# A recurrence in 32-frame chunks: values transposed for four chunks at a time, and operand copies placed behind the exponentials

## The chip, the core and the metric

The kernel runs on one core of a Trainium2 chip. The metric is the device time of one execution in microseconds; the time before is the median of three runs. A core has five engines that run side by side, each through a queue of its own in order: TensorE (PE in the profile, its weight loads PEld), VectorE (DVE), ScalarE (ACT), GpSimd (POOL) and SyncE (SP), which here only issues DMAs. Tiles lie in SBUF (128 partitions) or, where matmuls write, in the eight banks of PSUM.

## The reference, cut to what matters

One encoder block of width 1024 over 512 frames, all float32. Between two feed-forward halves stand two mixers; the change lies where both are computed side by side.

```python
def rwkv7_recurrence(r, w, k, v, a, b):
    # per head (8 heads of 64): S_t = S_{t-1} diag(w_t) + (S_{t-1} a_t) b_t^T + v_t k_t^T;  y_t = S_t r_t
    def step(state, inp):
        r_t, w_t, k_t, v_t, a_t, b_t = inp
        sa = jnp.einsum('bhvk,bhk->bhv', state, a_t)
        state = (state * w_t[:, :, None, :]
                 + sa[..., :, None] * b_t[:, :, None, :]
                 + v_t[..., :, None] * k_t[:, :, None, :])
        return state, jnp.einsum('bhvk,bhk->bhv', state, r_t)
    ...

def forgetting_attention(q, k, v, log_f):
    cum = jnp.cumsum(log_f, axis=-1)
    ...
    s = jnp.einsum('bhqd,bhkd->bhqk', q_i, k) * scale + c_i[..., :, None] - cum[..., None, :]
    pr = jax.nn.softmax(jnp.where(mask, s, -jnp.inf), axis=-1)
    return jnp.einsum('bhqk,bhkd->bhqd', pr.astype(v.dtype), v)

def reference(x, ...):
    x = x + 0.5 * swiglu(rms_norm(x, ffn1_norm), ...)
    p = rms_norm(x, mix_norm) @ w_in
    y_a = rwkv7_mixer(token_shift(p[..., :SHIFT_COLS]), ...) @ rwkv_proj
    y_b = fox_mixer(p[..., SHIFT_COLS:SHIFT_COLS + FOX_COLS], ...) @ fox_proj
    x = x + (gate_a * y_a + gate_b * y_b) @ w_out
    x = x + 0.5 * swiglu(rms_norm(x, ffn2_norm), ...)
    return rms_norm(x, final_norm)
```

## The kernel before

Activations lie with features on partitions and the 512 frames along the free dimension. Weights come in pieces from HBM (`raw`); each is split into a rounded half `whi` (a cast on ScalarE, line 133) and a remainder `wlo` (a subtraction on VectorE, line 134), and a wide product is three matmuls of 128x512, line 142. The program runs the first feed-forward half, the input projection, the scan (534 to 690 us), the output projections and the second half.

**The scan** (lines 1457 to 1539) runs the recurrence in 16 chunks of 32 frames, c = 0 to 15. The state of each pair of heads and the data that it meets lie in four sets of operands: `Rs` (64 rows of state, 32 rows of the solved values and 32 rows of V, by head) and `Ds`, both slices of the `RD` tiles. Chunk c uses set c % 4. Within a chunk TensorE makes, in this order:

- `xps`, what the state gives for the chunk's frames (issued by `read` at the end of the chunk before, line 1435), copied to `Xs` by VectorE;
- a staging transpose for two later chunks: in even chunks `stage_v` turns V (`vp`, line 1236, four transposes, one for each pair of heads) and ScalarE copies it in four copies into two sets `Rs` (line 1240); in odd chunks `stage_b` does the same for `Ds` (`bp`, lines 1245 and 1249);
- some of the wide products that are left over from the projections (`pq`, `pgt`, line 142), which fill the time;
- `ups`, the product with the chunk's inverse triangular matrix (line 1475), which ScalarE copies to `R` in four copies (lines 1479, 1480);
- more wide products, and the logits `lp` of one unit of the attention (lines 1308 to 1310);
- `sps`, the new state (line 1502), which VectorE scales by the decay into the next set (line 1504), and `yps`, the outputs (line 1508), copied over V by ScalarE (line 1512).

The attention works on 12 units, three for each pair of heads, spread over 12 of the chunks. For a unit VectorE takes maxima (`mx`, line 1318) and ScalarE exponentials (`pts`, line 1319) in one chunk; in the next, the weights are transposed by TensorE (line 1333), copied to `tr` (line 1338) and multiplied by the values (line 1347). Before a pair's first unit its queries and keys are squared, summed over a head (`pq2`, line 1161), rooted (`qrn`, lines 1165 and 1166) and scaled (line 1170), and `operands` copies them into the matmuls' operands (`qa`, `qb` on ScalarE, lines 1271 and 1272; `kb`, `klc` on VectorE). These copies, and the splits and evacuations of the wide products, stand in a list `side`, which `flush` empties at the start of each chunk.

The inverse triangular matrices are made ahead of the scan: 31 steps on VectorE (`TT`, lines 1122 and 1124), a DMA from ScalarE's queue to DRAM (`Td`, line 1125), and four DMAs back into `Tall` in another layout (line 1131), two on ScalarE's queue and two on GpSimd's.

`xps`, `vp`, `bp`, `ups`, `sps`, `yps` and most `pq2` share a pool `pr` of three PSUM banks, so that a new tile waits for the readers of the tile that had its bank before. The order of each engine's queue is set by a list scheduler when the program is built; what is marked `keep` stays in the order of the code, and `tc.issue_after(x)` puts the instructions of a block behind instruction x where both are on the same engine.

Of the kernel before, what the change touches and what calls it, by code (L numbers as in the profile page):

```python
# [9 lines left out]
F32 = mybir.dt.float32  # L10
F32R = mybir.dt.float32r
BF16 = mybir.dt.bfloat16
AF = mybir.ActivationFunctionType
# [5 lines left out]
P = 128  # L19
# [6 lines left out]
NP = DA // P  # L26
C = 32
NC = T // C
NB = T // P
# [22 lines left out]
def kernel(  # L52
# [7 lines left out]
    dve, act, pool, pe = nc.vector, nc.scalar, nc.gpsimd, nc.tensor  # L60
# [6 lines left out]
    pr = ctx.enter_context(tc.tile_pool(name="pr", bufs=3, space=PSUM))  # L67
# [11 lines left out]
    ident = cp.tile([P, P], F32, name="ident")  # L79
# [183 lines left out]
    with tc.tile_pool(name="x0", bufs=1) as x0:  # L263
        keep = tc.keep_in_program_order
# [436 lines left out]
    keep = tc.keep_in_program_order  # L701
# [180 lines left out]
    with ExitStack() as mx:  # L882
        rp = mx.enter_context(tc.tile_pool(name="rp", bufs=1))
        sctx = ExitStack()
        sp = sctx.enter_context(tc.tile_pool(name="sp", bufs=1))
# [48 lines left out]
        def normed(ps, rows=P):  # L934
            u = tmp("u")
            dve.tensor_tensor(u[0:rows, :], ps[0:rows, :], mix.rstd[0:rows, :], op=ALU.mult)
            return u

        u = normed(psa, 72)
        shifted(la, u, 64, PAR_MUA)  # L940
        dve.tensor_scalar(fz[64:72, :], u[64:72, :], pc(PAR_F)[64:72, :], None, op0=ALU.add)
        u = normed(psg, 96)
# [34 lines left out]
        vs = [V4[:, p] for p in range(NP)]  # L977
# [141 lines left out]
        for t in range(C - 1):  # L1119
            n, m = t + 1, C - 1 - t  # L1120
# [7 lines left out]
        for i in range(2):  # L1128
            for q in range(2):
                o = i * 64 + q * C  # L1130
# [59 lines left out]
        for b in range(NB):  # L1190
            o = vts[b]
# [30 lines left out]
        Rs, Ds = [RD[i // 2][:, i % 2] for i in range(4)], [RD[2 + i // 2][:, i % 2] for i in range(4)]  # L1222
        for q in range(2):
            pool.memset(Rs[0][half(q), :, q, :], 0.0)
            for i in range(4):
                o = (1 - q) * 64
# [3 lines left out]

        keep = tc.keep_in_program_order

        def stage_v(c, keep=keep):
            vp = pr.tile([P, NP, 2, 64], F32, tag="b", name="vp")
            for p in range(NP):
                keep(pe.transpose(vp[0:64, p].rearrange("p a b -> p (a b)"), vs[p][:, c * C:(c + 2) * C], ident[:]))
            for j in range(2):
                for q in range(2):
                    o = 32 + (1 - q) * 64
                    act.copy(Rs[(c + j) % 4][o:o + 32, :, q, :], vp[j * C:(j + 1) * C, :, q, :])  # L1240

        def stage_b(c, keep=keep):
            bp = pr.tile([P, NP, 2, 64], F32, tag="b", name="bp")
# [13 lines left out]
        def flush(budget):  # L1257
            while side and budget > 0:
                cost, do = side.pop(0)
                do()  # L1260
                budget -= cost
# [30 lines left out]
        class Unit:  # L1292
# [19 lines left out]
            def weights(s):  # L1312
                for q in range(2):
                    pt, mx = pts[:, q], pairs[s.p][2][q]
                    for b in s.bl:
                        n, mb = (b + 1) * P, mx[:, b:b + 1]
                        l = s.lps[q][:, s.at[b]:s.at[b] + n]
                        dve.tensor_reduce(mb, l, axis=AX.X, op=ALU.max, negate=True)
                        act.activation(pt[:, s.at[b]:s.at[b] + n], l, AF.Exp, bias=mb, accum_out=mx[:, NB + b:NB + b + 1])

            def scaled(s):
                for q in range(2):
# [103 lines left out]
        for part in (stage_v, stage_b):  # L1426
            part(0, lambda i: i)
        some_of = [(2, 1, 3), (3, 3, 2)] + [(2, 1, 3), (3, 1, 2), (4, 2, 2), (2, 1, 3), (2, 1, 3), (2, 1, 3)] + [(4, 2, 2), (2, 1, 3), (2, 1, 3), (2, 1, 3), (4, 3, 3), (2, 1, 3), (2, 1, 3), (2, 1, 3)]

        def read(c):  # L1430
            R = Rs[c % 4]
            xps = pr.tile([P, 2, 64], F32, tag="b", name="xps")
            for p, q in heads():
                o = (p // 2) * 64 + q * C
                keep(pe.matmul(xps[o:o + C, p % 2, :], G[p][q][:, c, 0, :], R[:, p, q, :], start=True, stop=True,
                               tile_position=(0, o)))
            Xs = sp.tile([P, 2, 64], F32, tag="Xs", name="Xs", bufs=2)
            return Xs, dve.tensor_copy(Xs[:], xps[:])
# [12 lines left out]
        def unit(n):  # L1451
            return units[places.index(n)] if n in places else None

        parted.extend((0, n, part) for n, part in enumerate(first_parts))
        with tc.issue_after(ahead.ins):
            Xs, taken = read(0)
        for c in range(NC):
            R, Rn, Dt = Rs[c % 4], Rs[(c + 1) % 4], Ds[c % 4]
            cs = slice(c * C, (c + 1) * C)
            u, v = unit(c - 1), unit(c)  # L1460
            n = some_of[c]
            late_logits = v and c == 12
            if c + 2 < NC:
                (stage_b if c % 2 else stage_v)(c + 2 - c % 2)
            with tc.issue_after(taken.ins):
                flush(100 if c in (1, 12) else 5)
            some(n[0])
            if u:
# [49 lines left out]
            if c + 1 < NC:  # L1518
                Xs, taken = read(c + 1)
# [249 lines left out]
```

## Time and profile before

| | before |
|---|---|
| median of three runs | 1140.15 us (1140.03 to 1140.36) |
| the profiled execution | 1140.51 us, its span 1138.8 us |
| granted TensorE clock over the span | 0.999 |
| scan | 534 to 690 us |

In the profile's groups an instruction stands with its line, engine and operation, output<-inputs, and sizes. In a timeline the columns are the start in us, the duration in us, engine, line, operation, tiles, sizes, the count of instructions merged, and in brackets how long the engine had been idle and what ended that. TensorE shows a float32 matmul of the recurrence as two, so that `xps` stands with x16 for 8 matmuls. The PE entries' durations overlap: the difference of two starts is what a matmul costs. A windows row gives start and end, the length, then busy time (and instructions) of PE, PEld, DVE, ACT and POOL, the granted clock, the DMA engines' share and GB/s. A waits row gives the engine and line that waited, who was waited for, the total, how often, and the longest. DMAs in a queue stand under ACTq and POOL.

### The profile page before, as it was taken

What the parts mean: (1) busy time and instruction counts of PE and PEld (TensorE: products, weight loads), DVE (VectorE), ACT (ScalarE), POOL (GpSimd) and SP (SyncE); (2) the same over time, 40 slices, a digit from 0 to 9 for tenths busy, and PEclk for the clock granted to TensorE, in tenths of its full rate; (3) what the DMA queues carried; (4) which work ended last, traced back from release to release, by engine and by line L of the source; (5) the groups of instructions that cost most, each with busy time, mean ns of one, the idle gap of its engine ahead of it and who ended that gap; (6) DMA issues with size and microseconds to landing.
All of it is one profiled execution on the core that took longest, in us unless ns stands there. A gap on an engine that the chain in (4) does not pass through costs nothing.

```text
span 1138.8 us, 19344 instructions
## 1 busy us (share of the span) xinstructions
PE 1127.8 (99%) x7674; PEld 988.1 (87%) x7674; DVE 830.0 (73%) x1301; ACT 600.9 (53%) x1004; POOL 106.8 (9%) x174
## 2 busy tenths in 40 slices
PE   9999999999999999999999999999999999999997
PEld 7899999988887888888777777888999999988887
DVE  6889999953246888777766668879999999943233
ACT  6645665532226754355877757536555566532121
POOL 2000000010111111321000011132000000010000
PEclk9999999999999999999999999999999999999999
DMA  8433333353334333345113236544333333363321
GB/s 260 135 93 109 97 112 111 95 181 115 112 103 124 103 104 103 112 142 139 38 38 100 67 113 200 177 142 126 103 97 108 111 94 112 107 192 91 89 78 74
DMA packets 210729, 131.14 MB, mean 115 GB/s; under 512 B 10415, under 2 KB 200943, under 8 KB 210639
## 3 DMA queue, kind: packets, MB, share of 16 engines
q1 hardware_dynamic: 202078, 108.67, 32.8%
q0 software_dynamic: 6320, 20.45, 5.4%
q8 instruction: 60, 0.98, 0.4%
q10 hardware_dynamic: 2240, 0.79, 0.3%
q14 instruction: 31, 0.25, 0.1%
HBM read 115.02 MB, written 14.88 MB: 114 GB/s over the span
## 4 chain that ended last, share of the span: by engine, by line
PE 96%; DVE 2%; ACT 1%; issue 1%; DVEq 0%; ACTq 0%
PE pd L142 21%; PE za L142 19%; PE zc L142 14%; PE pgt L142 8%; PE pk L142 6%; PE pw L142 4%; PE ppj L1553 4%; PE pb L142 3%; PE pa L142 3%; PE pq L142 3%; PE pv L142 2%; PE pl L142 1%; PE f L309 1%; PE gp L1076 1%; PE lp L1333 1%; PE lp L1347 1%
## 5 line engine op out<-in xcount | busy, mean ns | idle before, releaser
L133 ACT CAST whi<-raw 128x1024 fp32r<-128x1024 f32 (+3 forms) x117 | 113.8, 974 | 238.4 <-PE pd L142 153.7
L134 DVE TENSOR_TENSOR wlo<-raw,whi 128x1024 fp32r<-128x1024 f32 (+3 forms) x117 | 131.9, 1128 | 120.6 <-ACT whi L133 120.3
L142 PE MATMUL pd<-hh,wlo 128*128 128x512 f32 (+1 forms) x332 | 126.5, 381 | 0.0
L142 PE MATMUL pd<-hh,whi 128*128 128x512 f32 (+1 forms) x332 | 126.1, 380 | 0.0
L142 PE MATMUL pd<-hl,whi 128*128 128x512 f32 (+1 forms) x332 | 126.0, 379 | 0.0
L142 PE MATMUL zc<-xh,whi 128*128 128x256 f32 x296 | 83.8, 283 | 0.0
L142 PE MATMUL zc<-xl,whi 128*128 128x256 f32 x296 | 83.8, 283 | 0.0
L142 PE MATMUL zc<-xh,wlo 128*128 128x256 f32 x296 | 83.8, 283 | 0.0
L142 PEld LDWEIGHTS pd<-hl,whi 128*128 128x128 f32 x332 | 62.4, 188 | 12.0
L142 PEld LDWEIGHTS pd<-hh,whi 128*128 128x128 f32 x332 | 62.4, 188 | 11.7
L142 PEld LDWEIGHTS pd<-hh,wlo 128*128 128x128 f32 x332 | 62.4, 188 | 11.6
L142 PEld LDWEIGHTS zc<-xh,whi 128*128 128x128 f32 x296 | 56.8, 192 | 0.0
L142 PEld LDWEIGHTS zc<-xl,whi 128*128 128x128 f32 x296 | 56.8, 192 | 0.0
L142 PEld LDWEIGHTS zc<-xh,wlo 128*128 128x128 f32 x296 | 56.8, 192 | 0.0
L504 ACT CAST wtwo<-wsum 128x1024 fp32r<-128x1024 f32 x37 | 38.8, 1050 | 32.8 <-PE za L142 32.8
L142 PE MATMUL pgt<-xh,whi 128*128 128x512 f32 x128 | 53.0, 414 | 0.0
L507 DVE TENSOR_TENSOR wlo<-raw,whi 128x1024 fp32r<-128x1024 f32 x41 | 50.0, 1219 | 2.7 <-ACT whi L504 2.7
L516 DVE TENSOR_TENSOR wsum<-wsum,raw 128x512 f32<-128x512 f32 x74 | 50.9, 688 | 1.2
L516 DVE TENSOR_TENSOR wsum<-raw 128x512 f32<-128x512 f32 x74 | 50.6, 684 | 0.0
L142 PE MATMUL pgt<-xh,wlo 128*128 128x512 f32 x128 | 50.2, 392 | 0.0
L142 PE MATMUL pgt<-xl,whi 128*128 128x512 f32 x128 | 50.0, 391 | 0.0
L732 POOL DMA_DIRECT2D xP<-xpark x16 | 8.7, 548 | 438.2 <-PE za L142 437.5
(519 smaller groups left out, 3334.0 us busy)
## 6 DMA issues: line engine op xcount, KB each, us to landing
raw<-in_ffn_w_dram SPq DMA_DIRECT2D x118, 512.0 KB
raw<-in_w_in_dram SPq DMA_DIRECT2D x40, 512.0 KB
raw<-in_ffn_w_dram SPq DMA_DIRECT2D x15, 384.0 KB
xP<-xpark POOLq DMA_DIRECT2D x16, 256.0 KB, 4.7
raw<-in_w_out_dram SPq DMA_DIRECT2D x8, 512.0 KB
gsave<-gs SPq DMA_DIRECT2D x9, 256.0 KB
xin<-in_x_dram SPq DMA_DIRECT2D x4, 512.0 KB
xpark<-xT POOLq DMA_DIRECT2D x8, 256.0 KB, 6.3
```

What stands on the lines that cost most here:

```text
L133: marks["wide"] = act.copy(hi[:], raw[:])
L134: marks["rest"] = (eng or dve).tensor_tensor(lo[:], raw[:], hi[:].bitcast(F32), op=ALU.subtract)
L142: mm = pe.matmul(ps, w, x_, start=first and n == 0, stop=last and n == 2, skip_group_check=chain)
L309: return keep(pe.matmul(first[w][:], wt, x_[:], start=k == 0 and n == 0, stop=k == KD - 1 and n == 2))
L504: keep(act.copy(dst, src))
L507: keep(dve.tensor_tensor(dst, src, f32(hi), op=ALU.subtract))
L516: keep(dve.tensor_tensor(to, a, b, op=ALU.add))
L732: nc.gpsimd.dma_start(xT[c][:], xpark[c])
L1076: gm = pe.matmul(gps[g][o, c], BK[s, cc], G[p][q][s, cc], start=True, stop=True)
L1333: keep(pe.transpose(s.lps[q][:, k * P:(k + 1) * P], pts[:, q, k * P:(k + 1) * P], ident[:]))
L1347: keep(pe.matmul(av[half(q), j * P:(j + 1) * P], vt[k][:, h * 64:(h + 1) * 64], s.trs[q][:, o:o + P], start=k == 0, stop=k == b))
L1553: keep(pe.matmul(ps[:], a[:, k, :], y[k][b], start=k == 0 and n == 0, stop=k == NP - 1 and n == 2))
```

## The change

`stage_v` with c a multiple of four transposes V for four chunks (128 columns, so that `vp` fills all 128 partitions), copies the first two chunks' rows into `Rs` as before, and copies the upper 64 partitions of `vp` to a new SBUF tile `vkept` on VectorE. With the other even c it makes no transpose: ScalarE copies from `vkept` instead of `vp`. The second edit keeps, for each unit, its last exponential in `s.exp`, and puts what `flush` issues on ScalarE at the start of a chunk behind the last exponential of the unit of the chunk before.

```diff
+        vkept = []
+
         def stage_v(c, keep=keep):
-            vp = pr.tile([P, NP, 2, 64], F32, tag="b", name="vp")
-            for p in range(NP):
-                keep(pe.transpose(vp[0:64, p].rearrange("p a b -> p (a b)"), vs[p][:, c * C:(c + 2) * C], ident[:]))
+            if c % 4 == 0:
+                vp = pr.tile([P, NP, 2, 64], F32, tag="b", name="vp")
+                for p in range(NP):
+                    keep(pe.transpose(vp[:, p].rearrange("p a b -> p (a b)"), vs[p][:, c * C:(c + 4) * C], ident[:]))
+                src = vp
+            else:
+                src = vkept.pop()
             for j in range(2):
+                i = (c + j) % 4
                 for q in range(2):
                     o = 32 + (1 - q) * 64
-                    act.copy(Rs[(c + j) % 4][o:o + 32, :, q, :], vp[j * C:(j + 1) * C, :, q, :])
+                    act.copy(Rs[i][o:o + 32, :, q, :], src[i * C:(i + 1) * C, :, q, :])
+            if c % 4 == 0:
+                kept = sp.tile([P, NP, 2, 64], F32, name="vkept", tag="vkept")
+                dve.tensor_copy(kept[64:128], vp[64:128])
+                vkept.append(kept)
...
-                        act.activation(pt[:, s.at[b]:s.at[b] + n], l, AF.Exp, bias=mb, accum_out=mx[:, NB + b:NB + b + 1])
+                        s.exp = act.activation(pt[:, s.at[b]:s.at[b] + n], l, AF.Exp, bias=mb, accum_out=mx[:, NB + b:NB + b + 1])
...
-            with tc.issue_after(taken.ins):
+            with tc.issue_after(taken.ins), tc.issue_after(u.exp.ins) if u else ExitStack():
                 flush(100 if c in (1, 12) else 5)
```

The lines of the kernel after are numbered up to 11 higher than those before. In what follows, a row has its line, its operation, output<-inputs with the buffer's number, and the size of what is written.

TensorE, start of chunk 4, before: the last of `xps`, the transposes of V for chunks 6 and 7, and the wide products of a projection of the queries and keys (`pq`).

```order
L1435 MATMUL xps<-RD_5172,G_3630 32x64
L1435 MATMUL xps<-RD_5172,G_3631 32x64
L1236 MATMUL vp<-ident,V_3792 64x128 x4
L142 MATMUL pq<-xh_3591,whi 128x512
L142 MATMUL pq<-xl_3592,whi 128x512
```

The same place in the kernel after:

```order
L1446 MATMUL xps<-RD_5172,G_3630 32x64
L1446 MATMUL xps<-RD_5172,G_3631 32x64
L142 MATMUL pq<-xh_3591,whi 128x512
L142 MATMUL pq<-xl_3592,whi 128x512
L142 MATMUL pq<-xh_3591,wlo 128x512
```

The transposes are gone, and with them a tile of the pool `pr`; so it is in chunks 0, 8 and 12. Otherwise the order on TensorE is the same.

ScalarE, chunks 7 and 8, before: from the copies of chunk 7's `ups` to the table load that the first gate needs. `whi` and the four copies to `qa` and `qb` come from `flush`, the two exponentials are those of chunk 7's unit.

```order
L133 CAST whi<-raw 128x1024
L1338 COPY tr<-lp 128x384 x2
...
L1480 COPY RD_5173<-ups 32x2x64
L1271 CAST qa_6192<-qk_5395 64x512
L1272 CAST qb_5195<-qk_5395 64x512
...
L1319 ACTIVATE pts,mx_5721<-lp,mx_5721 128x512
L1319 ACTIVATE pts,mx_5722<-lp,mx_5722 128x512
L1165 ACTIVATE qrn<-pq_6140,epsr 128x512
L1166 ACTIVATE qrn<-qrn 128x512
L1512 COPY V_3792<-yps 128x4x32
L1371 ACT_TABLE_LOAD
L1371 ACTIVATE gs<-gs 128x512
L1240 COPY RD_5173<-vp 32x4x64 x4
```

The same stretch after:

```order
L1349 COPY tr<-lp 128x384 x2
...
L1491 COPY RD_5173<-ups 32x2x64
L1330 ACTIVATE pts,mx_5720<-lp,mx_5720 128x512
L1330 ACTIVATE pts,mx_5721<-lp,mx_5721 128x512
L133 CAST whi<-raw 128x1024
L1282 CAST qa_6188<-qk_5392 64x512
L1283 CAST qb_5195<-qk_5392 64x512
...
L1165 ACTIVATE qrn<-pq_6136,epsr 128x512
L1247 COPY RD_5173<-vkept 32x4x64
L1523 COPY V_3792<-yps 128x4x32
L1247 COPY RD_5173<-vkept 32x4x64
L1166 ACTIVATE qrn<-qrn 128x512
L1382 ACT_TABLE_LOAD
```

The cast and the operand copies have moved behind the exponentials, and two of the four copies for chunks 10 and 11 stand ahead of the table load (the other two stand earlier, in chunk 7). Chunks 3 and 4 have changed in the same way; in chunk 2 a `whi` has moved from ahead of the `tr` copies to behind the exponentials of that chunk.

ScalarE, ahead of the scan, before: the inverse's way through DRAM (`Td`, `Tall`), among the squares of the first pair (`qsq`, `shi`) and splits and evacuations.

```order
L133 CAST whi<-raw 128x1024
L1146 COPY qk_5044<-pq 128x512
L1125 DMA Td<-TT 128x1024
L1155 ACTIVATE qsq<-qk_4978 128x512
L1155 ACTIVATE qsq<-qk_5011 128x512
L157 CAST shi<-qsq 128x512 x2
L1131 DMA Tall<-Td 32x32x32 x2
L133 CAST whi<-raw 128x1024
L1146 COPY qk_5077<-pq 128x512
```

After:

```order
L133 CAST whi<-raw 128x1024
L1146 COPY qk_5044<-pq 128x512
L1247 COPY RD_5173<-vkept 32x4x64 x4
L1125 DMA Td<-TT 128x1024
L1155 ACTIVATE qsq<-qk_4978 128x512
L1155 ACTIVATE qsq<-qk_5011 128x512
L157 CAST shi<-qsq 128x512 x2
L133 CAST whi<-raw 128x1024
L1146 COPY qk_5077<-pq 128x512
L1131 DMA Tall<-Td 32x32x32 x2
```

The four copies for chunks 2 and 3, which stood behind the first `xps` of the scan, now stand ahead of `Td`, and `Tall` stands behind a cast and a copy. On VectorE the last step of the inverse has moved behind a `wlo`, before:

```order
L1122 TENSOR_TENSOR prod<-TT,Ls 128x31
L1124 TENSOR_TENSOR TT<-TT,prod 128x31
L1153 TENSOR_TENSOR qk_4978<-qk_4978,rstd 128x512
L1153 TENSOR_TENSOR qk_5011<-qk_5011,rstd 128x512
L1206 SCALAR_TENSOR_TENSOR nf<-la,nf 8x512
L134 TENSOR_TENSOR wlo<-raw,whi 128x1024
```

and after:

```order
L1122 TENSOR_TENSOR prod<-TT,Ls 128x31
L134 TENSOR_TENSOR wlo<-raw,whi 128x1024
L1124 TENSOR_TENSOR TT<-TT,prod 128x31
L1153 TENSOR_TENSOR qk_4978<-qk_4978,rstd 128x512
L1153 TENSOR_TENSOR qk_5011<-qk_5011,rstd 128x512
L1206 SCALAR_TENSOR_TENSOR nf<-la,nf 8x512
```

That `wlo` waits for the `whi` of the first row of the ScalarE listing.

## The prediction

> **What bounds the kernel now.** I read the page's busy shares first, then the chain that ended last, then the busy time of each engine in the stage that the change touches, which is the scan (534 to 690 us), and last TensorE's own waits there.
>
> ```profile
> span 1138.8 us, 19344 instructions
> PE 1127.8 (99%) x7674; PEld 988.1 (87%) x7674; DVE 830.0 (73%) x1301; ACT 600.9 (53%) x1004; POOL 106.8 (9%) x174
> ...
> PE 96%; DVE 2%; ACT 1%; issue 1%; DVEq 0%; ACTq 0%
> ```
>
> ```profile
> 534.00:690.00 156.00, 153.78 (x1620) 120.89 (x1619) 105.87 (x233) 119.77 (x303) 11.93 (x21) 1.00 0.27 81
> ```
>
> ```profile
> PE xps L1435 <- DVE RD L1504: 1.0, 4, 0.5
> ```
>
> The reader is to see that TensorE (PE) is the bound: 99% of the span, 96% of the chain. The scan is the one stage with something to collect, and it is little: in its 156.00 us TensorE is busy 153.78, VectorE (DVE) 105.87, ScalarE (ACT) 119.77. So two things make the kernel shorter here: fewer TensorE instructions, and fewer of the waits in the missing 2.2 us. The largest group of these waits, 1.0 us in four, is `xps` waiting for the decayed state of the chunk before; the change touches nothing in that chain. ScalarE, at 77% of the stage, is the engine to watch when its queue is put in another order.
>
> **The change part by part.** *Four transpose groups go.* `stage_v` is called eight times; of its groups of four transposes, those of chunks 2, 6, 10 and 14 (issued in chunks 0, 4, 8 and 12) are gone.
>
> ```profile
> 534.01 0.44 PE L1435 MATMUL xps<-RD,G 128*32 128x64 f32 x16
> 534.38 0.62 PE L1236 MATMUL vp<-ident,V 128*64 128x128 f32 x4
> 534.77 0.48 PE L142 MATMUL pq<-xh,whi 128*128 128x512 f32 x1
> 535.08 0.39 PE L142 MATMUL pq<-xl,whi 128*128 128x512 f32 x1
> ```
>
> ```profile
> 669.73 0.44 PE L1435 MATMUL xps<-RD,G 128*32 128x64 f32 x16
> ...
> 670.44 0.40 PE L142 MATMUL pgt<-xl,whi 128*128 128x512 f32 x1
> ```
>
> From the start of `xps` to the second wide matmul behind it, chunk 0 takes 535.08 - 534.01 = 1.07 us with a `vp` group between, and chunk 14, which has none, 670.44 - 669.73 = 0.71. The difference of starts, 0.36 us, is what a group costs (its 0.62 us of busy time overlap its neighbours). Four of them: **-1.44 us**, all on the path, since TensorE has no slack to absorb them.
>
> *The four groups that stay become wider*, 128 columns of V as weights in place of 64. No `vp` row shows that shape, but `bp`, the other staging transpose, has it.
>
> ```profile
> 542.64 0.66 PE L1245 MATMUL bp<-ident,BK 128*128 128x128 f32 x4
> 543.06 0.48 PE L142 MATMUL pq<-xh,whi 128*128 128x512 f32 x1
> ```
>
> ```profile
> L1236 PEld LDWEIGHTS vp<-ident,V x32: 108/111/113, 489.2 to 648.8; 128*64 128x64 f32 x32
> ...
> L1240 ACT COPY RD<-vp x32: 360/363/365, 497.1 to 650.3; 32x256 f32<-32x256 f32 x32
> ```
>
> ```profile
> L1245 PEld LDWEIGHTS bp<-ident,BK x32: 138/141/143, 495.2 to 661.3; 128*128 128x128 f32 x32
> ```
>
> A `bp` group takes 543.06 - 542.64 = 0.42 us from its start to the next matmul's, a `vp` group 534.77 - 534.38 = 0.39. So 0.03 a group, four groups: **+0.12 us**. The weight load itself grows from 111 to 141 ns; if none of that were covered it would be 16 x 30 ns = 0.48, which is the upper bound, and zero the lower.
>
> The Trainium skill, page "TensorE: Matmul & The Clock Gate", section on LDWEIGHTS, has a load's time grow with its columns, P / 1.2 ns. By that 64 more columns are 53 ns, 0.85 us for 16 transposes, and the sum below would be -1.14 instead of -1.87. The trace does not agree: its two loads differ by 30 ns, and the groups by 0.03 us.
>
> *A wait in chunk 4 goes.* The `vp` group of chunk 4 takes its PSUM bank over from the head sum whose root is `qrn`, and `qrn` stands on ScalarE behind a weight cast, four operand copies and two exponentials.
>
> ```profile
> 572.22 0.45 PE L1435 MATMUL xps<-RD,G 128*32 128x64 f32 x16
> 573.17 0.63 PE L1236 MATMUL vp<-ident,V 128*64 128x128 f32 x4 [0.51 <-ACT qrn L1165]
> ```
>
> From `xps` to `vp` are 0.95 us here against 0.37 in chunk 0: 0.58 lost. The group is gone, and the bank's next user is the state product `sps` at the end of chunk 4. **-0.58 us.** What is late next there is `qrn` itself, since the cast and the copies now stand between the exponentials and it; nothing asks for the bank before that `sps`, so this is free. If something did, 0.58 would come back.
>
> *A wait in chunk 2 goes.* The second logits matmul needs the bank that `tr` empties, and a weight cast `whi` stood ahead of `tr`.
>
> ```profile
> 555.91 1.03 ACT L133 CAST whi<-raw 128x1024 fp32r<-128x1024 f32 x1
> 556.97 0.48 ACT L1338 COPY tr<-lp 128x384 f32<-128x384 f32 x1
> ```
>
> ```profile
> 557.29 0.23 PE L1310 MATMUL lp<-dmask,identb 128*128 128x128 bf16 x1
> 557.50 0.45 PE L1308 MATMUL lp<-kb,qa 128*128 128x384 f32 x1
> ...
> 557.96 0.23 PE L1310 MATMUL lp<-dmask,identb 128*128 128x128 bf16 x1
> 558.00 0.48 PE L142 MATMUL pq<-xh,whi 128*128 128x512 f32 x1
> ```
>
> `tr` ends at 557.45 and the matmul starts at 557.50, 0.21 after its forerunner, where the like step costs 0.04. In the new order the cast stands behind the exponentials of chunk 2 and `tr` comes a microsecond sooner: **-0.17 us**. The casts themselves are hidden: the order of their remainders `wlo` on VectorE hardly moves, and each new place of a `whi` is still ahead of it.
>
> *The inverse is read back later.* The scheduler also moves rows ahead of the scan. The last step of the triangular inverse now waits on VectorE behind a `wlo`, and on ScalarE the four kept copies go ahead of the write `Td`, and a cast and a copy ahead of half of its reading back `Tall`.
>
> ```profile
> 523.01 1.05 ACT L133 CAST whi<-raw 128x1024 fp32r<-128x1024 f32 x1 [3.91 <-PE pq L142]
> 523.42 0.35 ACTq L1125 DMA_DIRECT2D Td<-TT  x1
> 523.97 0.58 ACT L1146 COPY qk<-pq 128x512 f32<-128x512 f32 x1
> ...
> 526.41 1.03 ACTq L1131 DMA_DIRECT2D Tall<-Td  x2
> ...
> 529.41 0.57 ACT L1146 COPY qk<-pq 128x512 f32<-128x512 f32 x1
> ```
>
> ```profile
> 525.28 1.23 DVE L134 TENSOR_TENSOR wlo<-raw,whi 128x1024 fp32r<-128x1024 f32 x1
> ```
>
> ```profile
> 526.68 1.60 POOL L1131 DMA_DIRECT2D Tall<-Td  x2 [2.34 <-DMA Td<-TT]
> ```
>
> ```profile
> DMA to landing us min/median/max: 6.2/6.2/6.3
> ```
>
> ```profile
> 537.27 0.46 PE L1475 MATMUL ups<-Xs,Tall 64*64 64x64 f32 x8
> ```
>
> VectorE: cast done at 524.06, `wlo` 1.23, the last step about 0.2, so 525.5. ScalarE: copy done at 524.55, four kept copies at 0.363 (the `vp` copies' price), so `Td` goes out at 526.0 in place of 523.42, 2.6 later. GpSimd's (POOL's) two reads follow it by the same: 529.3 and 530.1, landing at 536.3. ScalarE's two go out behind the copy that ends at 529.98. The first user, `ups`, comes at 537.27 - 0.36 = 536.9. So **0**, with 0.6 us left of a margin that was 3.6 (the before's last read landed at about 533.7); upper bound, with reads half a microsecond to one slower, +0.6.
>
> *ScalarE's fullest stretch becomes longer.* In chunks 7 and 8 its queue runs without a gap into the state copies that `sps` needs.
>
> ```profile
> 606.40 1.29 DVE L1318 TENSOR_REDUCE mx<-lp 128x1 f32<-128x512 f32 x2 [1.12 <-PE lp L1310]
> ```
>
> ```profile
> 606.81 0.61 ACT L1271 CAST qa<-qk 64x512 fp32r<-64x512 f32 x1
> ...
> 609.13 0.69 ACT L1319 ACTIVATE pts<-lp,mx 128x512 f32<-128x512 f32 x1
> ...
> 609.81 0.68 ACT L1319 ACTIVATE pts<-lp,mx 128x512 f32<-128x512 f32 x1
> ...
> 610.48 0.68 ACT L1165 ACTIVATE qrn<-pq,epsr 128x512 f32<-128x512 f32 x1
> ...
> 618.47 0.26 ACT L1480 COPY RD<-ups 32x128 f32<-32x128 f32 x1
> ```
>
> ```profile
> 619.14 0.34 PE L1502 MATMUL sps<-RD,RD 128*64 128x64 f32 x4
> ```
>
> Before, the copies end at 618.73 and `sps` starts at 619.14: 0.4 us of slack. Now the exponentials stand first and cannot start before the maxima: the second maximum is there at 607.69, its exponential done at 608.4. Then the cast (about 1.0), the operand copies (609.13 - 606.81 = 2.32), and the rest of the queue (618.73 - 610.48 = 8.25) with two kept copies in place of four `vp` copies (-2 x 0.363): 619.2. `sps` would come at 619.14 - 0.36 = 618.8, and its second half, which needs the last copies, a quarter of a microsecond later. **+0.2 us**, between 0 and 0.6. A kept copy is priced like a `vp` copy although its source is SBUF; no row shows that one, and the smaller copy from PSUM (0.26) and the operand cast from SBUF with twice the elements (0.61) bound it.
>
> The Trainium skill, page "VectorE: DVE Perf Modes", section on SBUF-source ops, puts ScalarE's fixed cost 52 cycles of 1.2 GHz higher from SBUF than from PSUM; by that two kept copies are 0.09 us longer and the sum is -1.78. No row before shows such a copy.
>
> *The four new copies on VectorE* (64x512 from PSUM to `vkept`; no row shows one, and the 1.23 of a `wlo` of twice the elements is a safe upper bound) cost nothing: those in the scan stand ahead of a wait for logits like the 1.12 in the row above; the first lies inside the inverse, whose end is set by the cast of 523.01. Without that cover they would delay the maxima by half of 1.23 each.
>
> Sum: -1.44 + 0.12 - 0.58 - 0.17 + 0 + 0.2 = **-1.87 us**. The profiled execution took 1140.51 (span 1138.8 and 1.7 around it), so 1138.64; the median of the runs, 1140.15, is 0.36 under it, so **1138.3**. That is 0.16%, and about 0.2% (2.3 us) is what a measurement of this kernel can tell from no change.
>
> **The rivals.** *The decay waits shrink too*: if less work ahead on ScalarE and VectorE let the state come sooner, the 1.0 us of `xps` waits goes as well: -2.87, 1137.3. Against it: in chunks without value products nothing but `sps` and its decay stands between, and neither is changed. *Only the transposes count*: the two waits come back elsewhere, since the queue is as full as before, or the moved rows are not ahead of what waits: -1.44 + 0.12 + 0.2 = -1.12, 1139.0. For it: ScalarE's 77%. Against: the banks' next users are far off. *The wider weight load shows in full*: 0.48 in place of 0.12, 1138.7; the groups of `bp` speak against it, and it is the page's rule on LDWEIGHTS in this kernel's numbers. *The inverse comes late*, the one way to slower: every microsecond that `Tall` lands after 536.9 stops TensorE for one at the first `ups`. If the reads took 9.3 us in place of 6.2, they land at 539.4, a stall of 2.5, and the kernel takes 1140.8. It outweighs the gain from a landing at 538.8 on, and is slower by 0.2% from 541.1. The margin of 0.6 speaks for it; against it, the DMA share of 0.27 in the scan leaves the reads room.
>
> **How the numbers follow.** Forecast 0.54, the decay waits 0.14, only the transposes 0.18, the full weight load 0.05, the late inverse 0.09. The range takes in the first two rivals, the full load, the bounds of the last two terms and the late inverse up to about no change: 1137.0 to 1140.2. Faster by over 0.2% (under 1137.87) needs the second case or the forecast at its lower edge, with no stall in chunk 8 and no wider transposes: 0.28. Slower by over 0.2% needs the late inverse at its worst: 0.05. Within: 0.67.
>
> **What would show it.** The scan's TensorE rows: `xps` directly followed by wide matmuls in chunks 0, 4, 8 and 12; `vp` groups at 0.42 from start to start; no wait for `qrn` in chunk 4 and no 0.21 step in chunk 2; the exponentials of chunk 7 done near 608 (less what TensorE has gained); `sps` of chunk 8 waiting 0.2 us or so for the copies; `Td` out near 526.0, `Tall` landing by 536.3 and `ups` not waiting. The forecast is wrong if `ups` waits, if chunk 8 waits more than 0.6, or if the scan's end moves by less than 1 us or more than 2.5.

## The result, and the profile after

| | before | after |
|---|---|---|
| median of 20 runs each | 1140.55 us (1140.03 to 1141.82) | 1138.56 us (1138.05 to 1139.72) |
| ratio, with its 95% interval | | 0.9982 (0.9976 to 0.9988) |
| profiled execution, its span | 1140.51, 1138.8 | 1139.03, 1137.3 |
| the scan, first to last `xps` | 144.83 us | 142.78 us |

The kernel is 1.99 us shorter, 0.18%; the forecast was 1.87. (The forecast of the time, 1138.3, started from a median of three runs of before, which lies 0.40 under that of the 20.) The page of the changed kernel, its busy shares, and the windows row of its scan (columns as before; the row begins at the first `xps` and ends at 689.20, so its length is not to be compared with the 156.00 of before):

```profile
span 1137.3 us, 19322 instructions
PE 1126.4 (99%) x7658; PEld 986.7 (87%) x7658; DVE 834.0 (73%) x1305; ACT 602.3 (53%) x1004; POOL 106.9 (9%) x174
```

```profile
534.63:689.20 154.57, 152.87 (x1606) 120.08 (x1606) 108.23 (x237) 120.03 (x300) 11.97 (x22) 1.00 0.27 83
```

TensorE has 16 matmuls fewer (the four groups), VectorE four copies more, 2.8 us; the rest has hardly changed. The profiled execution shows only 1.5 us of the 2.0, because the one of after began later: its first `xps` stands at 534.63, before's at 534.01, and the whole of that was there already at the first wide product (23.01 against 22.36). So the two traces are compared within the scan. TensorE's instructions have the same order in both, the `vp` groups aside (and two `yps` of chunk 8, which start ahead of the last `sps`). For each I take its start after minus its start before; where this shift changes, time was won or lost. It goes from +0.62 at the first `xps` to -1.43 at the last.

| place | forecast | change of the shift |
|---|---|---|
| chunks 0, 4, 8, 12: a group gone | -0.36 each | -0.38 each |
| chunks 2, 6, 10: wider group | +0.03 each | +0.03 each |
| chunk 2, second logits matmul | -0.17 | -0.17, and -0.02 at the next |
| chunk 4, wait for `qrn` | -0.58 | -0.58 (-0.96 with the group) |
| chunk 8, ahead of the logits | 0 | -0.10 |
| chunk 8, `sps` | +0.2 | +0.21 |
| scan | -1.87 (with the group ahead of it) | -2.05 |

The -0.38 of a group are read at the first wide product behind it. The second product gives 0.02 to 0.03 back, so that by the forecast's own measure, from `xps` to the second product, a group was worth 0.35 to 0.36. In `sps` of chunk 8 the shift rises by up to 0.27, at a late `yps`, and 0.06 of that come back at the next product; so the lasting loss is 0.21, where the expectations of two runs below speak of 0.25.

The rows of after that answer to those shown of before, on TensorE in chunks 0, 2, 4 and 8:

```profile
534.63 0.44 PE L1446 MATMUL xps<-RD,G 128*32 128x64 f32 x16
535.00 0.50 PE L142 MATMUL pq<-xh,whi 128*128 128x512 f32 x1
...
537.55 0.46 PE L1486 MATMUL ups<-Xs,Tall 64*64 64x64 f32 x8
...
557.64 0.23 PE L1321 MATMUL lp<-dmask,identb 128*128 128x128 bf16 x1
557.68 0.42 PE L1319 MATMUL lp<-kb,qa 128*128 128x384 f32 x1
...
572.36 0.45 PE L1446 MATMUL xps<-RD,G 128*32 128x64 f32 x16
572.74 0.50 PE L142 MATMUL pq<-xh,whi 128*128 128x512 f32 x1
...
617.87 0.84 PE L1513 MATMUL sps<-RD,RD 128*64 128x64 f32 x15
618.49 0.25 PE L1519 MATMUL yps<-G,RD 128*64 128x32 f32 x2
618.54 0.22 PE L1513 MATMUL sps<-RD,RD 128*64 128x64 f32 x1
```

Behind `xps` stands a wide product at once in chunks 0 and 4, 0.37 and 0.38 later; the second logits matmul of chunk 2 follows its forerunner by 0.04; and in chunk 8 the 16 matmuls of `sps` are drawn out to 0.84 us (0.69 where nothing is waited for), since they start one after another as ScalarE's copies of `ups` come in. These are on ScalarE, with what stands ahead of them:

```profile
606.23 0.69 ACT L1330 ACTIVATE pts<-lp,mx 128x512 f32<-128x512 f32 x1 [0.17 <-DVE mx L1329]
...
611.54 0.40 ACT L1247 COPY RD<-vkept 32x256 f32<-32x256 f32 x1
611.95 0.27 ACT L1523 COPY V<-yps 128x128 f32<-128x128 f32 x1
612.23 0.40 ACT L1247 COPY RD<-vkept 32x256 f32<-32x256 f32 x1
...
618.01 0.26 ACT L1491 COPY RD<-ups 32x128 f32<-32x128 f32 x1
```

No other row of this stretch has an idle time: from the exponential at 606.23, which waited 0.17 us for its maximum, to the end of the last copy at 618.27 the queue is full. The kept copies' prices, which no row of before showed, from the tile's view:

```profile
L1247 ACT COPY RD<-vkept x16: 400/403/407, 525.2 to 647.9; 32x256 f32<-32x256 f32 x16
L1250 DVE COPY vkept<-vp x4: 694/694/695, 499.3 to 632.1; 64x512 f32<-64x512 f32 x4
```

The inverse, its last step on VectorE and its write `Td`, before:

```profile
523.12 0.22 DVE L1124 TENSOR_TENSOR TT<-TT,prod 128x31 f32<-128x31 f32 x1
```

and after:

```profile
525.86 0.21 DVE L1124 TENSOR_TENSOR TT<-TT,prod 128x31 f32<-128x31 f32 x1
```

```profile
526.16 0.36 ACTq L1125 DMA_DIRECT2D Td<-TT  x1
526.43 0.41 ACT L1247 COPY RD<-vkept 32x256 f32<-32x256 f32 x1
```

`Td` goes out at 526.16, which is 525.54 on before's scale (forecast 526.0). It follows the end of VectorE's last step by 0.09 us, as before by 0.08. The four kept copies, which stand ahead of it in ScalarE's queue, did not hold it: the fourth starts 0.27 us later than the write. GpSimd's second read goes out at 531.4 and lands 4.2 us later, at 535.6. `ups` comes at 537.55 and does not wait.

### The profile page after: what moved, and what is told of

The parts are those of the page before. It is cut to its first block, busy times and chain, and to the rows that moved or that the text cites. A ratio compares the mean times of both kernels' runs of the same rounds, so it can differ in the third digit from the quotient of the medians.

```text
span 1137.3 us, 19322 instructions
## 1 busy us (share of the span) xinstructions
PE 1126.4 (99%) x7658; PEld 986.7 (87%) x7658; DVE 834.0 (73%) x1305; ACT 602.3 (53%) x1004; POOL 106.9 (9%) x174
## 4 chain that ended last, share of the span: by engine, by line
PE 97%; DVE 2%; DMA 1%; ACT 0%; issue 0%; SPq 0%; DVEq 0%
PE pd L142 21%; PE za L142 19%; PE zc L142 14%; PE pgt L142 8%; PE pk L142 6%; PE pw L142 4%; PE ppj L1564 4%; PE pq L142 3%; PE pb L142 3%; PE pa L142 3%; PE pv L142 2%; PE pl L142 1%; PE gp L1076 1%; PE sps L1513 1%; PE lp L1344 1%; PE f L309 1%
```

## The experiments

All are compared by the scan, first to last `xps`, each read from one profiled execution. How much the scan of one kernel differs from execution to execution was not tried; where an edit touches nothing, the shift between two of these traces stays the same within some 0.05 us over whole chunks. The times, whose ratios are to the kernel before, hardly tell effects under a microsecond apart.

**The transposes alone.** The second edit is undone.

```diff
-            with tc.issue_after(taken.ins), tc.issue_after(u.exp.ins) if u else ExitStack():
+            with tc.issue_after(taken.ins):
```

> The transposes of four chunks and the kept buffer alone; the operand copies stay ahead of the exponentials as in the kernel before. The measure is the scan from the first to the last xps matmul: 144.82 us before, 142.78 with both edits. Theory (each term belongs to the edit that the prediction gave it to): the four groups go, 0.38 each, the stall of 0.58 in chunk 4 goes with its group, the wider groups cost 0.03 each, and the 0.17 in chunk 2 and the 0.10 ahead of the logits in chunk 8 stay: -2.0, less what the state product of chunk 8 waits. If the full ScalarE queue makes that wait, it is 0.2 here too and the scan takes 143.0; if the new order makes it, it is 0 and the scan takes 142.8. Rival (the stall in chunk 4 left because of the order): it stays, and the scan takes 143.4 to 143.6. Time 1138.7 +- 0.3 by the theory, 1139.3 by the rival.

The scan took 143.85 us, the time 1139.59 (ratio 0.9991, 0.9982 to 1.0000). Neither case: chunks 0, 4 and 12 won what was expected (0.38, 0.96, 0.38), chunk 8's group too, and chunk 4's wait is gone without the second edit; but chunk 8 lost 1.06 that the changed kernel does not lose, in two places. On TensorE:

```profile
604.95 0.23 PE L1321 MATMUL lp<-dmask,identb 128*128 128x128 bf16 x1
605.37 0.50 PE L1319 MATMUL lp<-kb,qa 128*128 128x512 f32 x1 [0.20 <-ACT tr L1349]
...
611.14 0.45 PE L1446 MATMUL xps<-RD,G 128*32 128x64 f32 x16 [0.62 <-ACT qrn L1165]
```

and on ScalarE:

```profile
600.46 0.40 ACT L1247 COPY RD<-vkept 32x256 f32<-32x256 f32 x1
...
601.82 0.40 ACT L1247 COPY RD<-vkept 32x256 f32<-32x256 f32 x1
602.24 1.50 ACT L1260 COPY RD<-bp 64x256 f32<-64x256 f32 x4
603.77 1.05 ACT L133 CAST whi<-raw 128x1024 fp32r<-128x1024 f32 x1
604.84 0.86 ACT L1349 COPY tr<-lp 128x384 f32<-128x384 f32 x2
...
609.05 0.69 ACT L1330 ACTIVATE pts<-lp,mx 128x512 f32<-128x512 f32 x1
...
610.40 0.69 ACT L1165 ACTIVATE qrn<-pq,epsr 128x512 f32<-128x512 f32 x1
```

TensorE ends the first logits of chunk 8 1.2 us sooner than before (the row of 604.95 stood at 606.13; this trace began its scan 0.16 later), and ScalarE's queue is hardly earlier: the exponentials stand at 609.05 against 609.13 before, and `qrn` at 610.40 against 610.48. So `tr` (behind a cast) and `qrn` (behind four copies and the exponentials), which before were done 0.8 and 0.1 us ahead of the matmuls that need them, are now late: the second logits matmul comes 0.38 late and `xps`, which was given the bank that `qrn` reads, 0.68. Most of what was won in chunks 0 and 4 is given back in chunk 8, and then `sps` there finds ScalarE done and waits for nothing.

Part of the lateness is the first edit's own. Up to the `qrn` of the head sum before, ScalarE had kept pace (598.72 against 599.80 before). Then two kept copies, 0.40 each, stand ahead of the cast, where before all four copies stood behind the exponentials. In the run with these copies on GpSimd, below, ScalarE starts the same copies of `bp` 0.9 sooner than in the changed kernel, counted from the first `xps`. My estimate from these rows: with the two copies gone, some 0.8 of the 1.06 us would come back without the second edit. The first edit alone with its kept copies on GpSimd was not run.

**The order alone.** Before, with the second edit only.

```diff
... (s.exp kept as in the change)
-            with tc.issue_after(taken.ins):
+            with tc.issue_after(taken.ins), tc.issue_after(u.exp.ins) if u else ExitStack():
```

> The operand copies and weight casts behind the exponentials alone; vp is transposed for two chunks as before. Theory (the second edit needs the first): in chunk 4 the logarithm qrn, which holds the bank that vp takes, falls behind a cast and four copies, from 572.4 to about 573.4, so that vp's stall grows from 0.58 to about 1.6; the same in chunk 8 costs 0 to 0.5; 0.17 and 0.10 are gained in chunk 2 and ahead of chunk 8's logits. The scan takes 145.5 to 146.2 instead of 144.82, the time 1141.2 to 1142. Rival (the edits are independent): the scan takes 144.5, the time 1140.3, and the stall ahead of vp in chunk 4 stays 0.58.

The scan took 145.98 us, the time 1142.12 (ratio 1.0012, 1.0004 to 1.0021): slower, and the scan is as long as expected, but that was chance, for the parts were not. The 0.17 in chunk 2 came, the 0.10 ahead of chunk 8's logits did not. `vp` lost 0.39 more in chunk 4 (about 1.0 expected) and 0.96 in chunk 8 (0 to 0.5 expected), and for another reason. On TensorE in these two chunks:

```profile
571.91 0.44 PE L1435 MATMUL xps<-RD,G 128*32 128x64 f32 x16
573.25 0.63 PE L1236 MATMUL vp<-ident,V 128*64 128x128 f32 x4 [0.90 <-DVE Xs L1438]
...
611.29 0.45 PE L1435 MATMUL xps<-RD,G 128*32 128x64 f32 x16
612.64 0.63 PE L1236 MATMUL vp<-ident,V 128*64 128x128 f32 x4 [0.90 <-DVE Xs L1438]
```

The releaser, that is, what ended the wait, is not `qrn` but VectorE's copy `Xs`: with `qrn` later, `vp` was given another bank, that of the `xps` directly ahead of it, and waits until that is copied out. The program built from a kernel names the bank of each tile, and the two programs say the same: in chunk 4 `vp` has the bank of the head sum before, and with the second edit alone that of `xps`. The banks go with the scheduler's order, so that moving one reader changes which tile gets which bank. So the second edit by itself costs 1.15 us, the first by itself brings 0.98, and both together 2.05: with the groups of chunks 4 and 8 gone, nobody is left to wait where the order alone waits.

**All chunks but the eighth.** In the changed kernel chunk 8 keeps the order of before.

```diff
-... tc.issue_after(u.exp.ins) if u else ExitStack():
+... tc.issue_after(u.exp.ins) if u and c != 8 else ExitStack():
```

> The changed kernel, with chunk 8 alone left in the order of before (its cast and operand copies ahead of the exponentials). The state product of chunk 8 waited 0.25 for ScalarE's last copies of ups in the changed kernel. Theory (the queue is full: the same work in another order): the wait stays between 0.15 and 0.5, and the scan takes 142.8 to 143.1. Rival (the new order makes the wait): it goes, and the scan takes 142.5 to 142.6.

The scan took 143.65 us. Both cases were wrong, and the run says the same as the first: the two stalls of chunk 8 are back, and with TensorE 1.1 later `sps` waits no more.

```profile
606.33 0.50 PE L1319 MATMUL lp<-kb,qa 128*128 128x512 f32 x1 [0.19 <-ACT tr L1349]
612.08 0.45 PE L1446 MATMUL xps<-RD,G 128*32 128x64 f32 x16 [0.61 <-ACT qrn L1165]
```

**The eighth chunk alone.** The opposite cut.

```diff
-... tc.issue_after(u.exp.ins) if u else ExitStack():
+... tc.issue_after(u.exp.ins) if u and c == 8 else ExitStack():
```

> The transposes of four chunks, with the operand copies and the cast behind the exponentials in chunk 8 alone. With the transposes alone TensorE lost 0.38 in chunk 8 waiting for a copy tr behind a weight cast, and 0.68 ahead of xps waiting for the logarithm qrn, whose bank it was given. Theory (the second edit is worth what it does in chunk 8, 0.17 in chunk 2 aside): both stalls go, the scan takes 142.8 to 143.1. Rival (they depend on the order in the earlier chunks too): the scan takes 143.4 to 143.9.

The scan took 142.93 us, as the theory said, 0.15 over the changed kernel. Chunk 2 accounts for 0.12 of that. In chunk 8 the second logits matmul follows at once, and `xps` comes at 610.25 without a wait. So of the 1.07 us that the second edit brings on top of the first, 0.9 are won in this one chunk.

The two stalls do not go in the same way. The `tr` copies come sooner, since the cast stands behind them. But `qrn` is no earlier: counted from the first `xps` it starts at 76.35 here and at 76.19 in the changed kernel, against 76.23 with the transposes alone. `xps` does not wait for it because it has another bank: in the changed kernel it runs at 610.30, and `qrn` ends at 611.51. On the head sum's bank it would have come 1.2 us later by this estimate, and nearly all that the second edit brings in chunk 8 would be gone. The table has the banks in the programs built from six kernels. The traces agree: TensorE waits for a semaphore of ScalarE at this `xps` in the first three kernels and not in the last three:

| kernel | bank of chunk 7's head sum (read by `qrn`) | bank of chunk 8's `xps` |
|---|---|---|
| before | 4 | 4 |
| the transposes alone | 2 | 2 |
| all chunks but the eighth | 3 | 3 |
| changed | 3 | 2 |
| the eighth chunk alone | 2 | 3 |
| the order alone | 2 | 3 |

**The kept copies on GpSimd.** ScalarE is relieved of the 16 copies out of the kept buffer.

```diff
-                    act.copy(Rs[i][o:o + 32, :, q, :], src[i * C:(i + 1) * C, :, q, :])
+                    (pool.tensor_copy if c % 4 else act.copy)(Rs[i][o:o + 32, :, q, :], src[i * C:(i + 1) * C, :, q, :])
```

> The changed kernel, with the 16 copies out of the kept buffer on GpSimd instead of ScalarE, 0.40 us each there. Theory (chunk 8's queue is full): two of them stand ahead of the copies of ups in chunk 8, so ScalarE is 0.8 earlier and the wait of 0.25 goes; the scan takes 142.5. Rival (another instruction sets the wait, or GpSimd is late): GpSimd's copies take over 1 us each, or come later than the matmuls that read them, and the scan takes 142.8 or more. GpSimd's price for such a copy is in neither trace; its copies of 64x512 bound it only roughly.

The scan took 142.67 us. The wait ahead of `sps` is gone: its 16 matmuls take 0.69 again, and ScalarE's last copy ends at 617.07, 0.7 us ahead of them.

```profile
617.76 0.69 PE L1513 MATMUL sps<-RD,RD 128*64 128x64 f32 x16
```

```profile
L1247 POOL COPY RD<-vkept x16: 391/396/862, 525.2 to 646.8; 32x256 f32<-32x256 f32 x16
```

So the full queue made that wait, as forecast. The gain is 0.11 and not 0.21, since 0.08 is lost again ahead of the logits of chunk 8, where the 0.10 of the table was won; what stands behind that 0.1 was not followed further.

**The copy into the kept buffer, four times over.**

```diff
-                dve.tensor_copy(kept[64:128], vp[64:128])
+                for _ in range(4):
+                    dve.tensor_copy(kept[64:128], vp[64:128])
```

> The changed kernel with the copy into the kept buffer made four times over, 2.1 us more of VectorE at each of four places (one ahead of the scan). Theory (the kept copies are hidden with room to spare): the scan takes 142.7 to 142.9. Rival (VectorE's copies delay a decay, an Xs or the maxima): each of the three places inside the scan shows up to 2 us, and the scan takes 143.2 or more.

The scan took 143.11 us: 0.33 more, all of it at the `sps` of chunk 8, between the two cases. Neither chunk 2 nor chunk 10 lost anything for 2.1 us of VectorE each; in chunk 6 two maxima were pushed back, and with them ScalarE's exponentials, behind which its rows have no idle time up to the copies of `ups` in chunk 8. VectorE there:

```profile
593.46 1.42 DVE L1251 COPY vkept<-vp 64x512 f32<-64x512 f32 x2
594.92 0.56 DVE L1330 TENSOR_REDUCE mx<-lp 128x1 f32<-128x384 f32 x1
595.50 0.69 DVE L1251 COPY vkept<-vp 64x512 f32<-64x512 f32 x1
596.23 0.56 DVE L1330 TENSOR_REDUCE mx<-lp 128x1 f32<-128x384 f32 x1
```

In the changed kernel the one copy ends 0.72 us ahead of the maxima:

```profile
594.48 0.69 DVE L1250 COPY vkept<-vp 64x512 f32<-64x512 f32 x1
595.89 1.04 DVE L1329 TENSOR_REDUCE mx<-lp 128x1 f32<-128x384 f32 x2 [0.72 <-PE lp L1321]
```

So in the changed kernel the copies cost nothing, and the room in chunk 6 is one copy more.

**Work behind `yps`.** The four waits for the decayed state, 1.0 us by the view of waits and 1.4 with what TensorE loses around them, are open in both kernels. A wide product is moved into them.

```diff
-            some(n[2] if not late_logits else 0)
+            hold = 0 if u or c + 1 == NC else 1
+            some(n[2] - hold if not late_logits else 0)
...
+            some(hold)
```

> The changed kernel, and in the chunks without value products (0, 1, 5, 9) the last weight product is issued behind yps instead of ahead of sps, so that TensorE has 0.7 us of work while VectorE decays the state that xps reads. xps waited 0.37, 0.37, 0.34 and 0.37 there. Theory (these are the only waits at those places, and ScalarE's copies of ups are done 0.6 us or more before the earlier sps): all four go, the scan takes 141.3 to 141.5 instead of 142.78, the time is 1137.2. Rival (sps then waits for ScalarE instead, or a later bank or copy takes the time back): the scan takes 142.3 to 142.9.

The scan took 141.86 us, the time 1138.12 (ratio 0.9976, 0.9966 to 0.9985): 0.92 won of the 1.4, which lies between the two cases. Chunks 5 and 9 won 0.38 and 0.41; chunk 0 won 0.15, since VectorE's scaling of `qk` stands ahead of the decay; chunk 1 won nothing. There the second head sum waited for VectorE instead; the last run below shows that the decay, too, waits there for more than `sps`.

```profile
550.24 0.50 PE L1161 MATMUL pq<-slo,bonesr 128*128 128x512 f32 x1 [0.16 <-DVE slo L158]
```

**Both.** Work behind `yps`, and the kept copies on GpSimd.

> The same, with the 16 copies out of the kept buffer on GpSimd, which took 0.40 us each there and took 0.11 off the scan by themselves. Theory (the gains add): the scan takes 141.2 to 141.4, the time 1137.1. Rival (with TensorE earlier by 1.1 in chunk 8, ScalarE's queue limits it there and relieving it is worth more): e5 shows a wait of 0.4 or more ahead of chunk 8's sps, and this run is 0.4 or more below e5.

With the kept copies on GpSimd as well the scan took 141.78 us and the time was 1137.74 (0.9972, 0.9962 to 0.9982): 0.08 under the run before, where the GpSimd copies alone had won 0.11. `sps` of chunk 8 waited no longer. The gains add, the rival is out, and the forecast of 141.2 to 141.4 shares the error of the run before.

**Without chunk 1.** As the run before, with `hold = 1 if c in (0, 5, 9) else 0`.

> The changed kernel, with the copies out of the kept buffer on GpSimd, and the weight product behind yps in chunks 0, 5 and 9 only. In chunk 1 the run with all four won nothing: the second head sum waited 0.31 for VectorE's slo instead, xps started no earlier, and 0.05 was lost. Theory: the scan takes 141.7 (141.78 with all four), the time 1137.6 to 1137.9. Rival (chunk 1's earlier sps helped what follows): 142.1.

Without the product in chunk 1: scan 141.73 us, time 1137.64 (0.9976, 0.9966 to 0.9985), as the theory said. This is the shortest of the scans, 1.05 us below the changed kernel and 3.10 below the one of before; against the changed kernel the difference of the medians, 0.9 us, is inside what the intervals leave open.

**The head sums behind `yps`.** As the run before, and one edit more in chunk 1.

> The same, and in chunk 1 the two matmuls of the head sums stand behind yps instead of the product. Theory (0.47 us of work covers the wait of 0.37 ahead of xps): the scan takes 141.3 to 141.5. Rival (the order decides which bank a group is given): head sums, xps and vp now take the three banks in another turn; in the built program vp waits for the copy of yps, which ScalarE makes behind the exponentials of the chunk, so that vp stands 0.5 to 1.2 us and the scan takes 141.9 to 142.7.

```diff
-            ends = head_sums() if c - 1 not in (3, 7, 11) else None
+            ends = head_sums() if c - 1 not in (3, 7, 11) and c != 1 else None
...
+            if c == 1:
+                ends = head_sums()
```

The scan took 141.75 us: neither case. `vp` did not wait for the copy of `yps`, so the bank that it was given did no harm; and `xps` waited as before, with half a microsecond of work put ahead of it:

```profile
553.90 0.45 PE L1446 MATMUL xps<-RD,G 128*32 128x64 f32 x16 [0.36 <-DVE RD L1516]
```

```profile
552.21 0.77 DVE L1329 TENSOR_REDUCE mx<-lp 128x1 f32<-128x256 f32 x2 [0.33 <-ACT pts L1330]
552.91 0.85 DVE L1516 TENSOR_TENSOR RD<-sps,PC 64x256 f32<-64x256 f32 x2
```

In chunk 1 the decay follows VectorE's maxima, and the last two of these waited for an exponential on ScalarE; an earlier `sps` helps nothing there.

## Why the prediction was right, point by point

**The groups that go**: 0.36 a group was forecast from the difference of two chunks, and 0.35 to 0.36 measured between the same two instructions. **The wider groups**: 0.03 each, as the `bp` group had shown; the upper bound of 0.48 was far off. The load, from the tile's view:

```profile
L1239 PEld LDWEIGHTS vp<-ident,V x16: 137/141/143, 489.8 to 629.5; 128*128 128x128 f32 x16
```

The Trainium skill, page "TensorE: Matmul & The Clock Gate", section on LDWEIGHTS, has P / 1.2 ns for P columns, by which I estimate 53 ns for 64 more; the trace has 141 - 111 = 30 here as for `bp`, and so disagrees again.

**Chunk 4**: the 0.58 went, and nothing asked for the bank in time to bring it back; in the built program its next user is `sps` of chunk 4, as forecast. That the 0.58 belongs to the first edit is shown by the run of that edit alone, where it goes as well.

**Chunk 2**: 0.17 as forecast. The order alone wins the 0.17 too, the transposes alone 0.04; with the new order in chunk 8 alone, 0.12 of it are missing.

**The inverse**: `Td` was late by 2.1 us on the common scale (forecast 2.6), and there was no wait at `ups`; the rival with the late inverse is out. The forecast took the later of two times, VectorE's last step at 525.5 and ScalarE's copies at 526.0, and the second does not hold the write. The row of before says so already: `Td` went out at 523.42, and the copy that stands ahead of it in the queue started at 523.97. The margin came out at 1.9 us and not at 0.6, from errors that in part cancel: besides the earlier `Td`, GpSimd's first read went out 4.5 us behind it and not 3.3, and its reads took 4.2 us from issue to landing where before's took 6.2. (ScalarE's two reads have no landing in the trace.) In the run with the kept copies on GpSimd the last read landed at 537.16, only 0.2 ahead of `ups`.

**Chunk 8's `sps`**: forecast 0.2, measured 0.21, and the run with the copies on GpSimd shows that ScalarE's full queue makes it. The queue came out as added up: from `qrn` to the end of the last copy 7.45 us, against 8.25 - 0.73 = 7.52. The kept copies cost 0.403 us against 0.363 for those out of PSUM. The Trainium skill, page "VectorE: DVE Perf Modes", section on SBUF-source ops, has 52 cycles more for ScalarE from SBUF, by which I estimate 0.043 us; the trace agrees, with 0.040.

**The copies on VectorE**: hidden. VectorE idles 0.72 us behind the copy in chunk 6 and 0.47 in chunk 2; of the 2.1 us more that were put at each place, only those of chunk 6 reached TensorE, in chunk 8.

**The rivals**: the decay waits did not shrink: the view of waits of after has the same 1.0 us in four.

```profile
PE xps L1446 <- DVE RD L1515: 1.0, 4, 0.5
```

*Only the transposes count* came nearest to something real: its condition, a queue as full as before that takes the gain back, is what the first edit alone runs into. But in the changed kernel the moved rows prevent it: one stall goes by the earlier `tr`, the other by the bank that the new order gives to `xps`.

So the sum was right by its terms, and one thing beside them was overlooked without harm. The prediction priced the second edit at -0.17 in chunk 2 and +0.2 in chunk 8, about nothing. Alone it costs 1.15 us, and on top of the first it brings 1.07, nearly all in chunk 8. A term that is zero there, "two waits that do not appear", had no line in the sum, because I compared the new order with the waits of the kernel before, and not with the waits that the first edit's gain would have uncovered. That it did no harm was luck: nothing in the prediction looked at which bank `xps` of chunk 8 would get, and on the head sum's bank the changed kernel would by the estimate above have been about as slow as with the transposes alone, 1139.6.

What was not tried apart: no run held the order and changed the bank. That the bank decides whether `xps` waits is read from the built programs and the releasers of six kernels.

## What to carry to other kernels

Where one engine is the bound and another's queue is nearly as full, what is saved on the first must be followed down the program to the place where the second becomes the bound: saving 1.2 us of TensorE by chunk 8, and putting two copies more ahead on ScalarE, put `tr` and `qrn` 1.06 late there. After a change of order it pays to look up the new releaser of each wait, since the scheduler may have given a tile another bank. Two edits that look independent are then worth timing apart and together: here -0.98, +1.15 and -2.05. And in a kernel whose run-to-run spread is as large as the effect, the shift of one engine's instructions between two traces gives each term to a few hundredths.

## What the runs showed of the hardware

The first wide product of the program started between 22.00 and 23.97 us in the twelve traces of this case, and in the four traces where it started latest (23.01 and later) the transposes of the input ahead of it had waited for their loads. That row in the trace with the latest start, the one with the head sums moved:

```profile
9.42 1.09 PE L284 MATMUL xtp<-ident,xin 128*128 128x128 f32 x8 [1.40 <-DMA xin<-in_x_dram]
```

The later stages carry this start on: from the last `xps` to the start of TensorE's last instruction all twelve took 453.42 to 453.52 us. The 20 runs of either kernel lie 1.7 to 1.8 us apart; such a start would be enough to account for them, but only the profiled executions show theirs. So spans of single traces should not be compared where a microsecond matters.

GpSimd's copy of 32x256 float32 from SBUF to SBUF took 0.39 to 0.40 us in the scan, ScalarE's 0.40. GpSimd is busy for 12 of the scan's 154.6 us, so such copies can be moved there. But the four ahead of the scan took 0.76 to 0.86, beside VectorE's work on the inverse, and VectorE's last step of the inverse took 0.41 there where it took 0.21 in the changed kernel. All four traces with these copies on GpSimd show both; what makes it was not tried.

A DMA that stands in ScalarE's queue behind copies did not wait for them to start: `Td` went out 0.27 us ahead of the fourth kept copy, and in the kernel before 0.55 us ahead of the copy to `qk`.
